# Hybrid decoder step on one Trainium2 core: key choice of the sample rows placed ahead of the attention's steps

## The chip, the cores and the metric

The kernel runs on one core of one Trainium2 chip. The metric is the device time of one execution in microseconds (us); less is better. Five engines work beside each other: TensorE (PE; its weight loads are PEld in the rows), VectorE (DVE), ScalarE (ACT), GpSimd (POOL) and SyncE (SP, which here only issues transfers). Each engine takes its own instructions strictly in the order in which they were written into its stream, and waits on semaphores for the others.

## What is computed

One layer of a decoder, for a prompt of 512 rows and for 32 sample rows (8 sequences of 4) that share all weights. Cut to what matters:

```python
h = rmsnorm(x, norm_mix_g)
q, k, v, qi, ki, wi, xl, gl, ga, gb = split_cols(h @ w_in, IN_SPLITS)
q, k = rope(q), rope(k)
# attend: indexer scores -> top-256 keys of each row -> softmax attention on these keys only
y_a = attend(q, k, v, qi, ki, wi) @ w_proj_a
y_b = (rg_lru(causal_dwconv(xl)) * gelu(gl)) @ w_proj_b
x = x + (sigmoid(ga) * y_a + sigmoid(gb) * y_b) @ w_out
h = rmsnorm(x, norm_ffn_g)
ua, ub = split_cols(h @ w_up, (D_FF, D_FF))
x = x + (gelu(causal_dwconv(ua)) * ub) @ w_down
```

For a sample row `attend` picks 256 of 4096 cached keys by score, gathers their K and V rows (8 heads of 64) from a paged cache in DRAM, and attends to them and to the new rows of its own sequence.

## The kernel before

All large products are made in split precision: an operand is cut into a high and a low fp32r half (`split_act`, line 150 ff., for activations; `load_w`, line 161 ff., for weights: SP loads at L163, ACT casts at L166, DVE subtracts at L167), and three matmuls are added.

The order of the work is set by a tile scheduler: each piece of code has a priority (`tc.high_priority(n)`; more is earlier) and every engine's stream is written by these priorities as far as data allow. The places that matter here, in order of time:

- 200 to 365 us: q, k, v and index columns of the prompt (L232 to L234, priority PRIO) while DVE sorts the sample rows' scores for the 256 largest, 32 rounds of L782 and L784 (PRIO // 10).
- 300 to 420 us: the prompt's attention (PRIO // 3, the last unit 4 * PRIO): products with split keys (L545), scores and softmax (L950 on DVE, L955 and L959 on ACT), transposes (L965), products with V (L980). The gate rows and `w_proj_b` (L247 to L249, PRIO // 6) fill PE between its steps.
- The choice (L805 to L840, PRIO // 10): DVE compares all scores with the 256th (L810, L811), ranks ties by a scan (L813), PE counts (L815, L816), DVE selects (L818 to L823), a second count and scan number the keys (L825 to L829), ACT packs them (L830 to L832); SP writes the table `cbd` to DRAM (L834) and reads it back in another layout as `M` (`cw<-cbd`, L836); DVE takes the ends `se` from it (L838).
- The sample rows' q, k and v columns (L842 to L860, PRIO // 10): `sample_cols` loads four 512 KB pieces of `w_in` (L274, tiles `cg`) and makes 32 fp32 matmuls (L281; each shows as two in the profile's counts); q and k get rope (L376 to L380), a copy in DRAM (`qsd` for q) and transposes.
- 423 to 452 us: `w_proj_a` (L1022 to L1024, 3 * PRIO), eight blocks of 12 matmuls, each closed by DVE (L1025, L1026, L157). After each block stands one step of the generator `choose` (L866 to L890, PRIO // 10), whose 8 matmuls (L878) turn `M` into row numbers with DVE's L869, L870 and L882 to L889.
- 453 to 504 us: `w_out` (L1280 to L1282) and the sums with x (L1295).
- POOL gathers K and V rows by these numbers (L1055); it also makes the power in the second norm's rsqrt (L175), in one stream.
- From 504 us: the second norm (L183 to L192, transposes L202), then `w_up` and `w_down` (L260 to L262), between whose blocks the sample rows' attention is pinned step by step (L1082 to L1091, L1138), and the tail.

The step that hands the choice on to the gathers is:

```python
for ft in range(8):
    ...
    split_act(mhi[:, ft, :SEQ], mlo[:, ft, :SEQ], sg, 0.5)
    with tc.high_priority(PRIO // 10 - 3 * PRIO):
        next(chosen, None)
```

Of the kernel before, what the change touches and what calls it, by code (L numbers as in the profile page):

```python
# [96 lines left out]
def build(tc, I, O, dbg=None, mark=lambda n: None):  # L97
    nc = tc.nc
    V, S, T, G = nc.vector, nc.scalar, nc.tensor, nc.gpsimd
# [8 lines left out]
    def pool(stack, name, bufs, **k):  # L108
        return stack.enter_context(tc.tile_pool(name=name, bufs=bufs, **k))

    def maker(p, tag):
        return lambda shape=(128, 512), dt=F32: p.tile(list(shape), dt, tag=tag, name=nm(tag))

    with outer:
# [8 lines left out]
        PC = maker(pool(outer, "pc", 2, space=PSUM), "pc")  # L123
# [14 lines left out]
        def C(name, lo=0, hi=None):  # L138
            o, w = _OFF[name]
            return (cmk if name in _MASKS else cst)[:, o + lo:o + (w if hi is None else hi)]  # L140

        ident = C("ident")
# [3 lines left out]
        PRIO = 100000  # L146
# [149 lines left out]
        CW = maker(pool(mix, "cw", 6), "cw")  # L296
# [47 lines left out]
        b = PC()  # L344
# [24 lines left out]
        def rope(dst, src, n, t, nh, mk=None, adder=None):  # L369

            cs = C("cos", t * 64, t * 64 + 64)[:n, None, :].to_broadcast([n, nh, 64])
            sn = C("sin", t * 64, t * 64 + 64).rearrange("p (a d) -> p a d", a=2)[:n, None].to_broadcast([n, nh, 2, 32])
            t1, t2 = (mk or PW)(), (mk or PW)()
            a = t1[:n, :nh * 64].rearrange("p (h d) -> p h d", h=nh)
            b = t2[:n, :nh * 64].rearrange("p (h d) -> p h d", h=nh)
            V.tensor_tensor(a, src, cs, op=ALU.mult)  # L376
            V.tensor_tensor(b.rearrange("p h (a d) -> p h a d", a=2),  # L377
                            src.rearrange("p h (a d) -> p h a d", a=2)[:, :, ::-1, :], sn, op=ALU.mult)
            for d in (dst if isinstance(dst, list) else [dst]):
                (adder or V).tensor_tensor(d, a, b, op=ALU.add)  # L380

        def heads(ap):
            return ap.rearrange("p (h d) -> p h d", d=64)
# [32 lines left out]
        b = PC()  # L416
# [9 lines left out]
        b = PC()  # L426
# [6 lines left out]
        with tc.high_priority(3 * PRIO):  # L433
# [20 lines left out]
            for u in range(16):  # L454
# [19 lines left out]
                if g:  # L474
                    b = PA()
# [7 lines left out]
            b = PC()  # L483
# [7 lines left out]
            b = PC()  # L491
# [10 lines left out]
            qsT = mp.tile([128, 4, 32], F32, name="qsT")  # L502
            kTn = mp.tile([128, 4, 32], F32, name="kTn")
            vn = mp.tile([32, 512], F32, name="vn")
            qsd = dp.tile([NQ, 512], F32, name="qsd")

            def sample_cols(col0):
                return rows_by_columns(hs, 8, CG, w_in, col0, 8)
# [12 lines left out]
        for t in range(4):  # L521
            sl = slice(t * 128, (t + 1) * 128)
            qr = qrow[:, t]
            for c0, c1 in ((0, 256), (256, 584)):
                b = PD()[:, :c1 - c0]
# [8 lines left out]
        b = PD()  # L534
# [37 lines left out]
        with tc.high_priority(PRIO):  # L572
# [11 lines left out]
            b = PD()  # L584
# [59 lines left out]
            for k6 in range(6):  # L644
# [5 lines left out]
                b = PD()  # L650
# [98 lines left out]
        b = PD()  # L749
# [19 lines left out]
        with tc.high_priority(PRIO // 10):  # L769
            scr = CW((128, 1028), F16)  # L770

            def total(cnt, mat):
                b = PC()
                T.matmul(b[:, :1], mat, cnt, start=True, stop=True)
                return b[:, :1]


            rest, top = CG((128, 1028)), CW((128, 256))
            src = SC
            for r in range(32):  # L780
                with tc.issue_after(masked.ins):
                    V.max(top[:, 8 * r:8 * r + 8], src)  # L782
                if r < 31:
                    V.match_replace(rest, top[:, 8 * r:8 * r + 8], src, SENT)  # L784
                    src = rest


            def both(lists, n):
                other, u = CW((n, 256)), CW((n, 256))
                G.tensor_copy(other, lists[n:2 * n])  # L790
                V.tensor_tensor(u, lists[:n], other[:, ::-1], op=ALU.max)
                return u

            u = both(top, 64)
            for d in (128, 64, 32, 16, 8, 4, 2, 1):
                w = CW((64, 256))
                uv, wv = (t.rearrange("p (b a d) -> p b a d", a=2, d=d) for t in (u, w))
                for a, op in ((0, ALU.max), (1, ALU.min)):
                    V.tensor_tensor(wv[:, :, a], uv[:, :, 0], uv[:, :, 1], op=op)
                u = w  # L800
            u = both(u, 32)
            V.tensor_reduce(Ff[:32], u, axis=AX.X, op=ALU.min)
            for k in range(1, 4):
                G.tensor_copy(Ff[32 * k:32 * k + 32], Ff[:32])
        with tc.high_priority(PRIO // 10):  # L805

            eq = CG((128, 1028))
            gt = CG((128, 1028))
            cg, ce = SMC(), SMC()
            V.tensor_scalar(gt, SC, Ff, None, op0=ALU.is_gt, op1=ALU.add, accum_out=cg)  # L810
            V.tensor_scalar(eq, SC, Ff, None, op0=ALU.is_equal, op1=ALU.add, accum_out=ce)  # L811
            er = CG((128, 1028))
            V.tensor_tensor_scan(er, eq, eq, 0.0, ALU.add, ALU.max)  # L813
            b = PC()
            T.matmul(b[:, 0:1], C("sq"), cg, start=True, stop=False)  # L815
            T.matmul(b[:, 0:1], C("lq"), ce, start=False, stop=True)  # L816
            lim = SMC()
            V.tensor_scalar(lim, b[:, 0:1], -1.0, 256.0, op0=ALU.mult, op1=ALU.add)  # L818
            V.scalar_tensor_tensor(er, er, lim, eq, op0=ALU.is_le, op1=ALU.mult)
            sel = gt  # L820
            cs_ = cp.tile([128, 1], F32, name="cs_")
            V.scalar_tensor_tensor(sel[:, :1024], gt[:, :1024], 1.0, er[:, :1024], op0=ALU.mult, op1=ALU.add, accum_out=cs_)
            V.tensor_tensor(sel[:, 1024:], gt[:, 1024:], er[:, 1024:], op=ALU.add)  # L823
        with tc.high_priority(PRIO // 10):
            offs = cp.tile([128, 1], F32, name="offs")  # L825
            V.tensor_copy(offs, total(cs_, C("lq")))
            CB = CW((128, 8, 130), F16)
            V.tensor_copy(CB[:, :, 0], ptq_i)
            V.tensor_tensor_scan(eq[:, :1024], sel[:, :1024], sel[:, :1024], offs, ALU.add, ALU.max)  # L829
            S.copy(CB[:, :, 1:129], eq[:, :1024].rearrange("p (g s) -> p g s", g=8))  # L830
            S.copy(CB[:, 1:8, 129], CB[:, 0:7, 128])
            S.copy(CB[:, 0, 129:130], offs)  # L832
            cbd = dp.tile([NQ, NPG, 130], F16, name="cbd")
            nc.sync.dma_start(cbd.rearrange("q (c g) s -> c q (g s)", c=4), CB.rearrange("p g s -> p (g s)"))  # L834
            M = CW((128, 8, 130), F16)
            nc.sync.dma_start(M, cbd.rearrange("(b t) p s -> (t p) b s", b=8))  # L836
            se = cp.tile([128, 8, 2], F32, name="se")
            V.tensor_copy(se, M[:, :, 128:130])  # L838
            idx = {}
            scr2 = CW((128, 512), F16)  # L840
        with tc.high_priority(PRIO // 10):
            for col0, dstTs, rows in ((0, qsT, qsd), (512, kTn, O["k_s"])):  # L842
                b = sample_cols(col0)
                raw = CW((32, 512))
                for c in range(4):
                    S.copy(raw[:, c * 128:(c + 1) * 128], b[32 * c:32 * c + 32, :128])
                kr = CW((32, 512))
                rope(heads(kr), heads(raw), 32, 4, 8, CW)
                nc.scalar.dma_start(rows, kr)
                b = PC()  # L850
                for j in range(4):
                    T.transpose(b[:, j * 32:(j + 1) * 32], kr[:, j * 128:(j + 1) * 128], ident[:32, :32])
                S.copy(dstTs, b[:, :128].rearrange("p (k c) -> p k c", k=4))
            b = sample_cols(1024)
            for c in range(4):
                S.copy(vn[:, c * 128:(c + 1) * 128], b[32 * c:32 * c + 32, :128])
            nc.scalar.dma_start(O["v_s"], vn)
# [148 lines left out]
        with tc.high_priority(3 * PRIO):  # L1006
# [7 lines left out]
            for ft in range(8):  # L1014
# [4 lines left out]
                b = PD()  # L1019
# [462 lines left out]
        for _ in range(2):  # L1482
            raw = NM((128, 2, 512))
# [39 lines left out]
        for t in range(4):  # L1523
            b = PD()
# [8 lines left out]
            if t == 2:  # L1533
                first_half(4, NQ)
                b = PC()
# [43 lines left out]
```

## Time and profile before

| | |
|---|---|
| median of 3 runs | 1028.56 us (1028.41 to 1030.61) |
| the profiled execution: its time, its span | 1030.16 us, 1028.3 us |
| mean granted TensorE clock | 0.979 |
| PE busy | 976.0 us (95% of the span) |
| DVE busy | 719.6 us (70%) |
| ACT busy | 442.3 us (43%) |
| POOL busy | 206.2 us (20%) |

The busy shares are means over stages with different limits. PE is idle or at a lower clock in a few places only, so the time is read from those places: stretches of 25 us, then the instructions in them in order of time, with what ended the idle time ahead of each.

### The profile page before, as it was taken

How to read it: one execution, taken by the hardware profiler on the slowest of the kernel's cores; microseconds unless marked ns; L12 is line 12 of the kernel's file. 1: busy time of each engine (PE TensorE's matmuls, PEld its weight loads, DVE VectorE, ACT ScalarE, POOL GpSimd, SP SyncE). 2: the span in 40 equal slices, each digit the busy share in tenths (PEclk: the TensorE clock that was granted, in tenths of full speed). 3: DMA queues.
4: the chain of work that ended last, by engine and by line, in shares of the span. 5: the costliest groups of instructions: out<-in, count | busy, mean ns of one | idle time of the engine just before them, and what ended most of it. 6: DMA issues, size and time to landing. Idle time of an engine off the chain costs nothing.

```text
span 1028.3 us, 19018 instructions
## 1 busy us (share of the span) xinstructions
PE 976.0 (95%) x7342; PEld 800.2 (78%) x7342; DVE 719.6 (70%) x1557; ACT 442.3 (43%) x1104; POOL 206.2 (20%) x197
## 2 busy tenths in 40 slices
PE   4999999999999998899799999999999999999876
PEld 3977888987779987567588777776767889999655
DVE  5657898999999985576679878964444645554444
ACT  5233664742265555433546675642213223232233
POOL 3420000002200000004504746645651000000001
PEclk9999999999999999899889999999999999999989
DMA  7652222332332242996708887866784846764472
GB/s 265 216 159 70 84 63 73 95 107 83 123 103 84 84 130 68 287 321 214 236 29 235 277 252 233 283 204 189 241 264 157 297 125 226 235 215 152 148 245 88
DMA packets 144807, 178.95 MB, mean 174 GB/s; under 512 B 10620, under 2 KB 92668, under 8 KB 144716
## 3 DMA queue, kind: packets, MB, share of 16 engines
q1 hardware_dynamic: 119432, 109.24, 34.2%
q0 software_dynamic: 14688, 49.31, 14.2%
q10 hardware_dynamic: 10596, 19.18, 6.1%
q8 instruction: 58, 0.95, 0.4%
q14 instruction: 33, 0.27, 0.1%
HBM read 168.02 MB, written 9.68 MB: 173 GB/s over the span
## 4 chain that ended last, share of the span: by engine, by line
PE 75%; DVE 9%; issue 5%; DMA 4%; ACT 3%; POOL 3%; ACTq 0%; POOLq 0%; SPq 0%; DVEq 0%
PE pd L249 6%; PE pd L247 6%; PE pd L248 6%; PE pc L281 4%; PE pd L232 3%; PE pd L234 3%; PE pd L233 3%; POOL cg L1055 2%; PE pa L545 2%; PE pd L261 2%; PE pd L260 2%; PE pd L262 2%; PE pa L260 2%; PE pa L261 2%; PE pa L262 2%
## 5 line engine op out<-in xcount | busy, mean ns | idle before, releaser
L166 ACT CAST wh<-wr 128x1024 fp32r<-128x1024 f32 (+1 forms) x126 | 125.0, 993 | 219.2 <-PE pd L234 60.6
L167 DVE TENSOR_TENSOR wl<-wr,wh 128x1024 fp32r<-128x1024 f32 (+1 forms) x126 | 145.5, 1155 | 97.5 <-ACT wh L166 96.8
L247 PE MATMUL pd<-hhi,wh 128*128 128x256 f32 (+1 forms) x384 | 113.7, 296 | 0.1
L249 PE MATMUL pd<-hhi,wl 128*128 128x256 f32 (+1 forms) x384 | 112.7, 294 | 0.0
L248 PE MATMUL pd<-hlo,wh 128*128 128x256 f32 (+1 forms) x384 | 112.3, 293 | 0.0
L1055 POOL DMA_INDIRECT cg<-in_cache_k_dram,idx x64 | 76.0, 1188 | 151.8 <-DVE cw L870 94.9
L249 PEld LDWEIGHTS pd<-hhi,wl 128*128 128x128 f32 x384 | 72.3, 188 | 4.5 <-issue 4.0
L247 PEld LDWEIGHTS pd<-hhi,wh 128*128 128x128 f32 x384 | 72.3, 188 | 3.3 <-issue 1.8
L248 PEld LDWEIGHTS pd<-hlo,wh 128*128 128x128 f32 x384 | 72.3, 188 | 2.8 <-issue 2.7
L1055 POOL DMA_INDIRECT cg<-in_cache_v_dram,idx x48 | 55.0, 1146 | 28.5 <-ACT junk L1087 14.8
L175 POOL TENSOR_TENSOR smn<-smn,mhalf 128x1 f32<-128x1 f32 (+1 forms) x15 | 10.8, 722 | 241.0 <-DVE smn L1515 200.2
L261 PE MATMUL pd<-mlo,wh 128*128 128x512 f32 (+1 forms) x136 | 53.4, 393 | 0.1
L262 PE MATMUL pd<-mhi,wl 128*128 128x512 f32 (+1 forms) x136 | 53.2, 391 | 0.0
L260 PE MATMUL pd<-mhi,wh 128*128 128x512 f32 (+1 forms) x136 | 53.2, 391 | 0.0
L260 PE MATMUL pa<-mhi,wh 128*128 128x512 f32 (+1 forms) x136 | 52.6, 387 | 0.0
L262 PE MATMUL pa<-mhi,wl 128*128 128x512 f32 (+1 forms) x136 | 52.2, 384 | 0.0
L261 PE MATMUL pa<-mlo,wh 128*128 128x512 f32 (+1 forms) x136 | 52.2, 384 | 0.0
L1087 ACT ACTIVATE junk<-cg 128x64 f16<-128x64 f32 x160 | 41.0, 256 | 24.5 <-DVE cg L1082 11.7
L380 POOL TENSOR_TENSOR pw<-pw,pw 128x512 f32<-128x512 f32 x8 | 11.2, 1398 | 192.9 <-DVE pw L377 189.2
L1082 DVE TENSOR_TENSOR cg<-cg,xb 128x1024 f32<-128x1024 f32 x32 | 38.5, 1217 | 7.2 <-DMA cg<-in_cache_k_dram,idx 3.7
L782 DVE MAX8 cw<-cg 128x8 f32<-128x1028 f32 x32 | 39.3, 1227 | 0.3
L784 DVE MATCH_REPLACE8 cg<-cw,cg 128x1028 f32<-128x1028 f32 x31 | 37.6, 1212 | 0.0
(586 smaller groups left out, 2720.7 us busy)
## 6 DMA issues: line engine op xcount, KB each, us to landing
wr<-in_w_up_dram SPq DMA_DIRECT2D x48, 512.0 KB
wr<-in_w_in_dram SPq DMA_DIRECT2D x36, 512.0 KB
sw<-in_w_up_dram SPq DMA_DIRECT2D x32, 512.0 KB
wr<-in_w_down_dram SPq DMA_DIRECT2D x20, 512.0 KB
xb<-qsd ACTq DMA_DIRECT2D x32, 256.0 KB
sw<-in_w_down_dram SPq DMA_DIRECT2D x16, 512.0 KB
cg<-in_w_in_dram SPq DMA_DIRECT2D x12, 512.0 KB
wr<-in_w_out_dram SPq DMA_DIRECT2D x8, 512.0 KB
```

The costliest lines, as they stand in the source:

```text
L166: S.copy(hi, raw)
L167: V.tensor_tensor(lo, raw, hi, op=ALU.subtract)
L247: T.matmul(b, hi[:, k, :], a_hi[:, k, c0:c1], start=k == 0, stop=False)
L248: T.matmul(b, hi[:, k, :], a_lo[:, k, c0:c1], start=False, stop=False)
L249: T.matmul(b, lo[:, k, :], a_hi[:, k, c0:c1], start=False, stop=k == nk - 1)
L260: T.matmul(b[:, c0:c1], hi[:, k, :], a_hi[:, k, c0:c1], start=k == 0, stop=False)
L261: T.matmul(b[:, c0:c1], hi[:, k, :], a_lo[:, k, c0:c1], start=False, stop=False)
L262: newest[0] = T.matmul(b[:, c0:c1], lo[:, k, :], a_hi[:, k, c0:c1], start=False, stop=k == 7)
L281: m = T.matmul(b[32 * c:32 * c + 32, :128], a_s[:, k, :], rows[k - k0][:, c * 128:(c + 1) * 128], start=k0 == 0 and k == order[0], stop=k1 ...
L782: V.max(top[:, 8 * r:8 * r + 8], src)
L1055: G.indirect_dma_start(out=dst[j], out_offset=None, in_=src, in_offset=IndirectOffsetOnAxis(ap=idx[q // 16, q % 4][:, j, q // 4 % 4:q // 4 ...
L1087: S.activation(junk, kt[:, j, h * 64:(h + 1) * 64], AF.Copy, accum_out=sT[:, g, j, q16, h:h + 1])
```

## The change

The code that picks the keys (L805 to L840) gets priority PRIO // 2 in place of PRIO // 10, which is above that of the prompt's attention (PRIO // 3). The loop over q and k columns becomes a function, `sample_heads`; its call for the q columns stands ahead of the choice (still PRIO // 10), the k and v columns stay behind it. No computation is added or removed. From L856 on a line of the changed kernel is 3 higher than before (L878 becomes L881); within the choice L815, L816 become L829, L830, and L838 becomes L852.

```diff
+        def sample_heads(col0, dstTs, rows):
+            b = sample_cols(col0)
+            raw = CW((32, 512))
+            for c in range(4):
+                S.copy(raw[:, c * 128:(c + 1) * 128], b[32 * c:32 * c + 32, :128])
+            kr = CW((32, 512))
+            rope(heads(kr), heads(raw), 32, 4, 8, CW)
+            nc.scalar.dma_start(rows, kr)
+            b = PC()
+            for j in range(4):
+                T.transpose(b[:, j * 32:(j + 1) * 32], kr[:, j * 128:(j + 1) * 128], ident[:32, :32])
+            S.copy(dstTs, b[:, :128].rearrange("p (k c) -> p k c", k=4))
         with tc.high_priority(PRIO // 10):
+            sample_heads(0, qsT, qsd)
+        with tc.high_priority(PRIO // 2):
 
             eq = CG((128, 1028))
...
-        with tc.high_priority(PRIO // 10):
+        with tc.high_priority(PRIO // 2):
             offs = cp.tile([128, 1], F32, name="offs")
...
         with tc.high_priority(PRIO // 10):
-            for col0, dstTs, rows in ((0, qsT, qsd), (512, kTn, O["k_s"])):
-                b = sample_cols(col0)
...
+            sample_heads(512, kTn, O["k_s"])
             b = sample_cols(1024)
```

PE, the first count of the choice. Before, it stands behind the last matmuls of the filler (tile `pd_5083`), next to the last attention unit (`pa_5163`):

```order
L247 MATMUL pd_5083<-hbhi,wh_5086 128x288
L248 MATMUL pd_5083<-hblo,wh_5086 128x288
L249 MATMUL pd_5083<-hbhi,wl_5087 128x288
L815 MATMUL pc_3129<-smc_3123,cst 128x1
L816 MATMUL pc_3129<-smc_3124,cst 128x1
L545 MATMUL pa_5163<-khi,pw_5160 128x256
```

Now it stands some 100 rows earlier on PE, at the seam of two filler blocks (`pd_4989` and `pd_5024`):

```order
L968 MATMUL pa_4324<-cst,pw_4241 128x128 x4
L249 MATMUL pd_4989<-hbhi,wl_4993 128x288
L815 MATMUL pc_3174<-cst,cw_3167 128x32
L829 MATMUL pc_3188<-smc_3182,cst 128x1
L830 MATMUL pc_3188<-smc_3183,cst 128x1
L247 MATMUL pd_5024<-hhi_135,wh_5028 128x256
```

The count moved over the last gate and `w_proj_b` blocks, and a transpose of the sample rows' q (`pc_3174`) stands just ahead of it.

DVE, the last attention unit (`pw_5160` is its split q, `pw_5177` its scores). Before, the second scan of the choice (L829) stands in it:

```order
L950 ISA sma_5178 128x1
L826 COPY offs<-pc_3139 128x1
L952 TENSOR_SCALAR sma_5179<-sma_5178 128x2
L829 SCALAR_TENSOR_TENSOR cg_3121<-cg_3122,offs 128x1024
L956 RECIPROCAL sma_5181<-sma_5180 128x2
L950 ISA pw_5190,sma_5191<-pa_5164,cst 128x128
```

Now the taking of `se` stands there, ahead of the split of q, and then the k columns' rope and the first step of `choose`:

```order
L154 TENSOR_TENSOR yalo<-qT,yahi 128x4x128 x2
L852 CAST se<-cw_3209 128x16
L154 TENSOR_TENSOR yalo<-qT,yahi 128x4x128
L154 TENSOR_TENSOR pw_5160<-qT,pw_5160 128x256
L959 RECIPROCAL sma_5151<-sma_5150 128x2
L376 TENSOR_TENSOR cw_3261<-cw_3255,cst 32x512
L377 TENSOR_TENSOR cw_3262<-cw_3255,cst 32x512
```

The select and scan of the choice left this stretch, and a wait for the read of `cbd` (tile `cw_3209` is `M`) came into it.

POOL, the gathers ahead of the second norm's first power (`smn_6061`), as a piece of the difference:

```order
+L1058 DMA cg_5861<-in_cache_k_dram,idx_5339 128x512 x2
+L1058 DMA cg_5907<-in_cache_k_dram,idx_5391 128x512 x2
 L175 TENSOR_TENSOR smn_6061<-smn_6059,mhalf 128x1
-L1055 DMA cg_5907<-in_cache_k_dram,idx_5391 128x512 x2
 L175 TENSOR_TENSOR smn_6088<-smn_6086,mhalf 128x1
```

Two gathers that stood behind the first power stand ahead of it; otherwise POOL's order is as it was.

## Rows read from the trace of the kernel before

**Rows 1.** The page: busy time, share of the span and instructions of each engine.

```profile
PE 976.0 (95%) x7342; PEld 800.2 (78%) x7342; DVE 719.6 (70%) x1557; ACT 442.3 (43%) x1104; POOL 206.2 (20%) x197
```

**Rows 2.** Busy time by stretch of 25 us: engines, granted clock, DMA share, GB/s.

```profile
225.00:250.00 25.00, 23.65 (x105) 18.61 (x104) 24.36 (x40) 5.37 (x6) 5.23 (x4) 1.00 0.30 86
400.00:425.00 25.00, 17.60 (x157) 12.46 (x157) 13.61 (x44) 13.42 (x44) 0.00 (x0) 0.80 0.57 177
425.00:450.00 25.00, 25.00 (x176) 17.35 (x178) 18.51 (x34) 9.54 (x19) 0.00 (x0) 1.00 1.00 334
500.00:525.00 25.00, 18.35 (x110) 14.33 (x109) 19.62 (x85) 12.45 (x47) 7.86 (x10) 0.73 0.32 96
```

**Rows 3.** DVE in order of time: start, us, engine, line [idle <-releaser].

```profile
383.33 2.29 DVE L813 TENSOR_TENSOR_SCAN cg<-cg 128x1028 f32<-128x1028 f32 x1
```

**Rows 4.** The choice on PE and DVE, same view, at the attention's end.

```profile
404.13 0.28 PE L815 MATMUL pc<-smc,cst 128*128 128x1 f32 x2
...
406.00 1.28 DVE L819 SCALAR_TENSOR_TENSOR cg<-cg,smc,cg 128x1028 f32<-128x1028 f32 x1
...
409.34 1.22 DVE L822 SCALAR_TENSOR_TENSOR cg<-cg,cg 128x1024 f32<-128x1024 f32 x1
...
411.55 2.35 DVE L829 TENSOR_TENSOR_SCAN cg<-cg,offs 128x1024 f32<-128x1024 f32 x1
```

**Rows 5.** The same view of PE: last attention unit, q columns, first w_proj_a.

```profile
409.47 0.79 PE L545 MATMUL pa<-khi,pw 64*128 64x256 f32 x4 [1.81 <-DVE pw L154]
...
414.24 1.93 PE L281 MATMUL pc<-cg,hs 128*32 128x128 f32 x30 [2.00 <-DMA cg<-in_w_in_dram]
...
422.72 0.72 PE L1022 MATMUL pd<-yahi,wh 128*128 128x512 f32 x2 [1.11 <-ACT yahi L153]
```

**Rows 6.** The same view of SP: the table written and read back.

```profile
416.47 0.61 SPq L834 DMA_DIRECT2D cbd<-cw  x1
...
426.26 0.37 SPq L836 DMA_DIRECT2D cw<-cbd  x1
```

**Rows 7.** The same view of DVE: se taken.

```profile
432.91 0.17 DVE L838 CAST se<-cw 128x16 f32<-128x16 f16 x1
```

**Rows 8.** The same view of PE: v columns inside w_proj_a.

```profile
449.32 1.08 PE L281 MATMUL pc<-cg,hs 128*32 128x128 f32 x32
```

**Rows 9.** The chain that ended last, in w_out: start, us, engine, line.

```profile
495.12 0.23 PE pd L1282
495.35 0.23 PE pd L1280
```

**Rows 10.** Groups on DVE from 453 to 526 us: count, busy us, mean ns.

```profile
L882 DVE TENSOR_SCALAR_CACHE_REDUCE cw<-pc,cst 128x127 f16<-128x127 f32 x32 | 9.5, 342 | 0.0
...
L1082 DVE TENSOR_TENSOR cg<-cg,xb 128x1024 f32<-128x1024 f32 x3 | 3.6, 1219 | 2.9 <-DMA cg<-in_cache_k_dram,idx 2.9
L1044 DVE COPY cw<-qsT 64x16 f32<-64x16 f32 x16 | 2.8, 176 | 0.2
```

**Rows 11.** POOL in order of time: gathers and the first power.

```profile
474.95 0.99 POOL L1055 DMA_INDIRECT cg<-in_cache_k_dram,idx  x1 [94.85 <-DVE cw L870]
...
488.52 1.96 POOL L1055 DMA_INDIRECT ft<-in_cache_v_dram,idx  x1 [0.30 <-issue]
...
502.99 0.95 POOL L1055 DMA_INDIRECT cg<-in_cache_k_dram,idx  x1 [0.30 <-issue]
504.00 0.57 POOL L175 TENSOR_TENSOR smn<-smn,mhalf 128x1 f32<-128x1 f32 x1
```

**Rows 12.** DVE in order of time: the first mean of squares of the second norm.

```profile
497.41 0.15 DVE L176 TENSOR_SCALAR smn<-smn 128x1 f32<-128x1 f32 x1
```

**Rows 13.** PE in order of time from the end of w_out.

```profile
504.53 0.63 PE L878 MATMUL pc<-cw,cw 32*128 32x128 f16 x8
506.39 1.09 PE L202 MATMUL pa<-cst,yn 128*128 128x128 f32 x8 [1.24 <-DVE yn L192]
...
526.53 0.39 PE L260 MATMUL pa<-mhi,wh 128*128 128x256 f32 x1
```

More of the change, by code (lines that the diff above doesn't have):

```diff
@@ L841, in build @@
         with tc.high_priority(PRIO // 10):
-            for col0, dstTs, rows in ((0, qsT, qsd), (512, kTn, O["k_s"])):
-                b = sample_cols(col0)
[L844 to L853, printed above, removed]
+            sample_heads(512, kTn, O["k_s"])
             b = sample_cols(1024)
```

## The prediction

> **What bounds the kernel now.** I read the page first. PE is busy for 976.0 us, 95% of the span [rows 1], and the change adds and removes no work, so only the places where PE stands still or runs at its lower clock can give time, and only places where PE is full can take it. The stretches of 25 us show them [rows 2]: 400 to 425 us (PE 17.60 of 25, granted clock 0.80) and 500 to 525 us (18.35, clock 0.73; a mean of 0.73 is a mixture of the two levels, 1.2 and 2.4 GHz). In 225 to 250 us PE has 1.35 us free, with DVE at 24.36 of 25. In 425 to 450 us PE has none.
>
> Then I read each place in order of time. The choice has its tie scan on DVE at 383.33 [rows 3], yet its first count on PE comes at 404.13 [rows 4]: its data have been there for 18.5 us, and it stands behind the filler in PE's stream. So its select, second select and second scan (406.00, 409.34, 411.55: 1.28 + 1.22 + 2.35 = 4.85 us of DVE, [rows 4]) fall into the attention's last unit, where PE starves (409.47, 414.24 and 422.72 all follow a wait, [rows 5]). From there the delay is handed on: the table goes out at 416.47 and is read back from 426.26 [rows 6], `se` is taken at 432.91 [rows 7], and the first gather starts at 474.95 [rows 11]. So gathers run on until 503.94 on POOL, and the second norm's first power stands behind them at 504.00 [rows 11], though its mean was there at 497.41 + 0.15 = 497.56 [rows 12]. PE ends `w_out` at 504.5, waits for the normalized rows at 506.39, and reaches steady FFN work only at 526.53 [rows 13]: 22.0 us, in which DVE also does the late steps of `choose`. That hole is what the change can close.
>
> **The change part by part.**
>
> (a) *q columns ahead.* 32 matmuls, 64 in the profile's count. 32 of that count last 1.08 us [rows 8], so 2.2 us, now among the prompt's q columns near 247 us, where PE has 1.35 us free in 25. Their four loads are issued by SP behind a weight load, at about 240 us by the order, and the last one is used first; the one row of such a wait is 2.00 us [rows 5]. Bounds 0.9 (the free time covers the rest) and 4.2. I take +2. The rope falls beside the attention, where DVE has room.
>
> (b) *The attention's tail.* The 4.85 us of DVE leave it. In come the taking of `se`, the k columns' rope, the first `choose` operations, and k and v columns on PE in place of the q columns, with their loads. The gain is at most 4.9. The loss hangs on the table: with the count near 389 us (the end of its filler block) the table is written at about 400.5; before, 16.4 us passed from its issue to `se` [rows 6, 7]. The same delay would put `se` at 416.9, and behind `se` on DVE stands the split of q for the last unit, which PE used at 409.47 [rows 5]: +7.4. Before, however, the read stood behind other transfers on SP and DMA was full (share 1.00, [rows 2]); now it stands ahead of them. Bounds -4.9 and +7.4; I take 0.
>
> (c) *k and v columns leave the full stretch* behind 422.72. 128 of the profile's count at 1.08 / 32 us each [rows 8]: 4.3 us less; both bounds are this, as PE had no idle time to hide them [rows 2]. I take -4.
>
> (d) *`choose` matmuls enter it.* Before, some 40 of them ran in the hole behind `w_out`; 8 last 0.63 us [rows 13], so +3 in `w_proj_a` and `w_out`.
>
> (e) *DVE beside `w_proj_a` and `w_out`.* From the first block to the third weight split of `w_out`, PE has by the new order 149 large matmuls at 0.23 us [rows 9] and 56 small: 34.9 + 4.4 = 39.3 us. DVE was busy 18.51 of 25 there [rows 2], or 29 us of 39. The order adds 23 counts of `choose` (0.34), 3 K products and 2 equally long reductions (1.22 each), 16 copies (0.18) [rows 10], 7.8 + 6.1 + 2.9 = 16.8 us, less some 2 us of k rope: 44 us. So DVE comes some 5 us late with a weight split. Bounds 0 (overlapped issue makes a count cheaper than its row) and +8; I take +4.
>
> (f) *The hole behind `w_out`.* `choose` is done in step with the blocks, so the first gather starts some 12 us of DVE work after 422.7, near 436, and the 22 gathers ahead of the first power, 0.95 + 0.30 us each [rows 11], end near 464, long before 497.6. The two that moved ahead of the power cost nothing under that cover; without it, 2.5 us. The hole keeps its own PE work: four times 1.09 us of transposes [rows 13] and 24 matmuls of half the width of `w_out`'s, 0.115 us each (an estimate from [rows 9]), 2.8 us. So at most 22.0 - 4.4 - 2.8 = 14.8 us go; at least 504.00 - 497.56 = 6.4 go, the wait of the power alone. With the path from the last sum to the last transposes still there, I take -12.
>
> Sum: 2 + 0 - 4 + 3 + 4 - 12 = -7 against the profiled execution, 1030.16: 1023. That execution lies 1.6 us above the median of 1028.56, so on the median's footing the forecast is **1021.5 us**. What is late next is the last row tile of the norm, then the FFN's own stalls.
>
> **Rivals.**
>
> *The gathers are slow beside a busy DVE, and still stand before the power.* In favour: where DVE was full, gathers of 1.96 us stand beside those of 0.95 [rows 11]. Against: 22 at 1.96 + 0.30 us take 50 us, from 436 to 486, in time for 497.6; it decides only if the first comes after 448. Then the power stays late, (f) keeps only the cleared `choose` steps, 12 - 6.4 = 5.6, and the time is 1028. The Trainium skill, "SBUF — State Buffer", section "SBUF: two separate sides", says that GpSimd cannot write the descriptors of its transfers while VectorE holds their shared port pair, and gives 3100 ns for a transfer that takes 620 ns alone; the 1.96 us rows agree in kind, not in size. By the page's figure, as an estimate, 22 gathers would take 68 us, end at 504, and the power would come no earlier than before.
>
> *Slower: the read of the table holds the attention's last unit.* One place, `se` on DVE ahead of the last split of q; on SP the loads of the v columns stand behind the same read. If it lands as late as it did (+7.4 in (b)), q's loads are late too (4.2 in (a), 2.2 more) and PE spends longer at the lower clock (2 more, an estimate from the 0.80 in [rows 2]), the sum is -7 + 7.4 + 2.2 + 2 = +4.6: 1033. It decides from about 7 us of lateness, `se` at 416.5. For it: the order and the 16.4 us. Against: that time held a queue that is now behind the read.
>
> *DVE takes the bound of `w_proj_a` and `w_out`.* (e) at +8 and (f) at its least: 2 - 4 + 3 + 8 - 6.4 = +2.6, 1031. For it: 44 us against 39. Against: later weight splits leave DVE room again before the norm.
>
> *The FFN gives it back.* The steps of the sample rows are pinned between its blocks and still want the same gathers; starting earlier, PE waits there instead. Half of the 7: 1025; all: 1028.5. Against: as many gathers are ahead of the norm as before.
>
> That the change does not do what it says is excluded for the order, which shows the count moved; that it moves no wait is the last rival.
>
> **How the numbers follow.** A difference under 0.2%, 2.1 us, cannot be told from no change here. Forecast (1012 to 1026): 0.60. Slow gathers: 0.05. Table: 0.15. DVE: 0.10. FFN: 0.10. Faster takes the forecast, half of the FFN's chance and a third of the gathers' and DVE's: 0.70. Slower takes the table's and a third of DVE's: 0.18; the rest, 0.12, is the same. The best sum, with every term at its gain, is 0.9 - 4.9 - 4.3 + 3 + 0 - 14.8 = -20, the worst beyond +10; neither end needs all its terms at once, so the range is 1011 to 1032, which cuts off half of the table's chance and little else.
>
> **What would show it.** PE's count near 389 us; `cbd` near 400 and `se` before 410; no select or scan of the choice after 404; first gather at 430 to 445; the first power within 1 us of its mean; the hole from `w_out`'s end to steady FFN at 8 to 12 us in place of 22.0, with the clock at 1.00 soon after. It is wrong if the attention's last products wait for `se`, if PE waits for `w_out`'s weight splits by over 8 us, or if the power still starts right behind a gather.

## The result and the profile after

Measured side by side, the changed kernel takes 1024.36 us (median of 5 runs, 1020.53 to 1025.65) and the kernel before 1030.07 us (1028.41 to 1030.74): a ratio of 0.994, interval 0.9922 to 0.9959, so 4 to 8 us faster. The forecast was 1021.5 in 1011 to 1032. The profiled execution of the changed kernel takes 1021.81 us, span 1020.0, granted clock 0.987; against the profiled one of before, 1030.16 and 1028.3, that is 8.3 us less. It lies 2.5 us under its own median, so the account below is of 8.3 us, while by the medians the change is worth 5.7. What follows reads these two traces.

The page: the same instructions, and PE 9.2 us less busy than in [rows 1], though it has the same matmuls; that fits the higher clock of 500 to 525 us below.

```profile
PE 966.8 (95%) x7342; PEld 796.3 (78%) x7342; DVE 720.1 (71%) x1557; ACT 441.4 (43%) x1104; POOL 208.9 (20%) x197
```

Busy time by stretch, columns as in [rows 2], of the changed kernel:

```profile
400.00:425.00 25.00, 17.82 (x224) 13.50 (x223) 12.34 (x46) 15.06 (x50) 0.00 (x0) 0.86 0.55 164
425.00:450.00 25.00, 23.47 (x114) 16.89 (x111) 18.12 (x65) 11.08 (x39) 4.55 (x5) 0.93 0.55 163
450.00:475.00 25.00, 19.33 (x93) 13.66 (x92) 22.55 (x65) 11.67 (x54) 17.96 (x16) 1.00 1.02 383
475.00:500.00 25.00, 24.14 (x112) 18.71 (x111) 14.58 (x39) 12.40 (x39) 1.89 (x2) 1.00 0.73 245
500.00:525.00 25.00, 23.81 (x146) 20.32 (x145) 16.57 (x37) 9.69 (x17) 2.22 (x4) 1.00 0.13 37
```

500 to 525 us, which stood at 18.35 us and clock 0.73, is repaired. A new weak stretch stands at 450 to 475 us: PE 19.33 of 25 at the full clock, with DVE at 22.55 and the DMA engines at a share of 1.02.

In order of time (start, us, engine, line, idle before and its releaser), the choice and the attention's last unit, PE, DVE and SP of the changed kernel:

```profile
390.62 0.38 PE L829 MATMUL pc<-smc,cst 128*128 128x1 f32 x2
...
398.35 2.35 DVE L843 TENSOR_TENSOR_SCAN cg<-cg,offs 128x1024 f32<-128x1024 f32 x1
...
402.75 0.61 SPq L848 DMA_DIRECT2D cbd<-cw  x1
...
410.66 0.37 SPq L850 DMA_DIRECT2D cw<-cbd  x1
...
413.82 0.17 DVE L852 CAST se<-cw 128x16 f32<-128x16 f16 x1 [4.39 <-DMA cw<-cbd]
414.51 0.42 DVE L154 TENSOR_TENSOR pw<-qT,pw 128x256 fp32r<-128x256 f32 x1
...
414.98 0.79 PE L545 MATMUL pa<-khi,pw 64*128 64x256 f32 x4 [5.10 <-DVE pw L154]
...
426.56 0.73 PE L1025 MATMUL pd<-yahi,wh 128*128 128x512 f32 x2 [1.11 <-ACT yahi L153]
```

The count is 13.5 us earlier than in [rows 4] and the second scan ends before 401. But `se` waits 4.39 us for the read of the table, the split of q stands behind it, and PE waits 5.10 us for that split where it waited 1.81 [rows 5]. `w_proj_a` starts at 426.56, 3.84 us later.

POOL of the changed kernel, the gathers and the first power of the second norm, and PE's first steady FFN product:

```profile
444.23 1.14 POOL L1058 DMA_INDIRECT cg<-in_cache_k_dram,idx  x1 [66.84 <-DVE cw L885]
...
467.10 1.65 POOL L1058 DMA_INDIRECT cg<-in_cache_k_dram,idx  x1 [0.30 <-DVE sT L1094]
...
481.21 0.94 POOL L1058 DMA_INDIRECT cg<-in_cache_k_dram,idx  x1 [8.68 <-ACT junk L1090]
482.46 0.95 POOL L1058 DMA_INDIRECT cg<-in_cache_k_dram,idx  x1 [0.30 <-issue]
502.39 0.57 POOL L175 TENSOR_TENSOR smn<-smn,mhalf 128x1 f32<-128x1 f32 x1 [18.99 <-DVE smn L183]
...
520.70 0.39 PE L260 MATMUL pa<-mhi,wh 128*128 128x256 f32 x1
```

The gathers end at 483.4, and the power, which stood behind one in [rows 11], now has 18.99 us of idle POOL before it. The last `w_out` matmul ends at 512.8, and steady FFN work comes 7.9 us later, in place of 22.0 [rows 13].

PE's waits from 427 to 515 us (us in total, times, longest) say why 450 to 475 us is weak:

```profile
PE pa L1284 <- DVE wl L167: 1.8, 1, 1.8
PE pc L881 <- ACT slot L890: 1.5, 1, 1.5
PE pa L1283 <- ACT wh L166: 1.4, 2, 0.8
PE pd L1025 <- ACT yahi L153: 1.1, 1, 1.1
PE pd L1027 <- DVE wl L167: 0.9, 2, 0.7
PE pc L881 <- DVE slot L889: 0.8, 1, 0.8
```

Both casters of the weights (ACT `wh`, DVE `wl`) are late, and both slot steps of `choose`. From the first `w_proj_a` matmul to the start of the last of `w_out` ("the stage" from here on) it takes 85.8 us, before 81.5.

What the stage is made of can be counted on PE, each row from its start to the start of the next, less the idle time (from the first start to the last end, 81.9 us before and 86.3 now). The k and v columns, with two groups of transposes (of q and k), took 8.0 us before and none now; `choose` 2.3 and 5.3; the large matmuls 70.9 and 72.5; eight transposes of the second norm, which stood behind `w_out`, 0 and 0.8; two small groups (L902, L903) 0 and 0.7; idle time 0.6 and 6.9. The columns were dear because they stood in pieces between the large matmuls. Here, before, ten of their count hold PE for 0.55 us until the next row starts, where [rows 8] has 32 in one piece of 1.08:

```profile
429.13 0.62 PE L281 MATMUL pc<-cg,hs 128*32 128x128 f32 x10
429.68 0.50 PE L1022 MATMUL pd<-yahi,wh 128*128 128x512 f32 x1
```

And the stage of the changed kernel begins at the lower clock. Its large matmuls start 0.43 us apart until 430.4 and 0.23 apart behind it; the granted clock is 0.59 from 426.5 to 430.6 and 0.99 in the 4.4 us that follow. Before, they started 0.23 apart from 423.8 on, at a clock of 1.00.

```profile
428.31 0.63 PE L1025 MATMUL pd<-yahi,wh 128*128 128x512 f32 x1
428.74 0.63 PE L1026 MATMUL pd<-yalo,wh 128*128 128x512 f32 x1
...
431.02 0.40 PE L1026 MATMUL pd<-yalo,wh 128*128 128x512 f32 x1
431.25 0.39 PE L1027 MATMUL pd<-yahi,wl 128*128 128x512 f32 x1
```

### The profile page after: what moved, and what is told of

The parts are those of the page before. It is cut to its first block, busy times and chain, and to the rows that moved or that the text cites. A ratio compares the mean times of both kernels' runs of the same rounds, so it can differ in the third digit from the quotient of the medians.

```text
span 1020.0 us, 19017 instructions
## 1 busy us (share of the span) xinstructions
PE 966.8 (95%) x7342; PEld 796.3 (78%) x7342; DVE 720.1 (71%) x1557; ACT 441.4 (43%) x1104; POOL 208.9 (20%) x197
## 4 chain that ended last, share of the span: by engine, by line
PE 77%; DVE 8%; DMA 6%; issue 3%; ACT 3%; POOL 1%; SPq 0%; ACTq 0%; POOLq 0%; DVEq 0%
PE pd L249 7%; PE pd L247 7%; PE pd L248 7%; PE pc L281 3%; PE pd L232 3%; PE pd L234 3%; PE pd L233 3%; PE pa L545 2%; PE pd L260 2%; PE pd L261 2%; PE pd L262 2%; PE pa L260 2%; PE pa L262 2%; PE pa L261 2%; PE pc L448 2%
## 5 line engine op out<-in xcount | busy, mean ns | idle before, releaser
L166 ACT CAST wh<-wr 128x1024 fp32r<-128x1024 f32 (+1 forms) x126 | 125.0, 993 | 225.3 <-PE pd L234 59.8
L249 PE MATMUL pd<-hhi,wl 128*128 128x256 f32 (+1 forms) x384 | 112.6, 294 | 0.0
L1058 POOL DMA_INDIRECT cg<-in_cache_k_dram,idx x64 | 80.7, 1261 | 126.0 <-DVE cw L885 66.8
L249 PEld LDWEIGHTS pd<-hhi,wl 128*128 128x128 f32 x384 | 72.2, 188 | 3.7 <-issue 3.0
L1058 POOL DMA_INDIRECT cg<-in_cache_v_dram,idx x48 | 51.3, 1068 | 26.5 <-ACT junk L1090 12.6
L1090 ACT ACTIVATE junk<-cg 128x64 f16<-128x64 f32 x160 | 41.0, 256 | 33.3 <-DVE cg L1085 15.6
```

The costliest lines, as they stand in the source:

```text
L166: S.copy(hi, raw)
L249: T.matmul(b, lo[:, k, :], a_hi[:, k, c0:c1], start=False, stop=k == nk - 1)
L1058: G.indirect_dma_start(out=dst[j], out_offset=None, in_=src, in_offset=IndirectOffsetOnAxis(ap=idx[q // 16, q % 4][:, j, q // 4 % 4:q // 4 ...
L1090: S.activation(junk, kt[:, j, h * 64:(h + 1) * 64], AF.Copy, accum_out=sT[:, g, j, q16, h:h + 1])
```

## The experiments

Ratios are to the kernel before in the same series, with 95% intervals. Times inside come from each kernel's profiled execution; one execution differs from the next by several us (the twelve of e1 lie between 1020.06 and 1033.48), so stages are compared inside executions, and small differences between kernels are left open.

**Which half of the change does it?** `e1_priority_only` is the kernel before with only the two priorities of the choice raised; `e2_q_columns_only` is the changed kernel with the choice back at its old priority.

```diff
-        with tc.high_priority(PRIO // 10):
+        with tc.high_priority(PRIO // 2):
```

> The priority of the choice alone, q columns left where they were in the program (behind the choice). Theory: the gain comes from the hole behind w_out, and that needs only the early choice; so the first gather stands near 440 us, the hole is 8 to 10 us, and the time is 1020 to 1027, with no q columns among the prompt's q columns and all three sets of columns in the attention's tail. Rival: the q columns are needed ahead (K products wait for q rows), then over half of the gain is gone, 1027 to 1030.

Measured: 1025.25 us, 0.9963 (0.9939 to 0.9986). The count comes at 384.06, `se` at 409.23 after a wait of 5.53 us, and PE waits 6.26 us: for ACT's half of q's split (L153), which stands behind a softmax step that waits 5.55 us for DVE, which stands at `se`. Hole from `w_out` to steady FFN 9.7 us; stage 83.4 us.

> The q columns ahead alone, choice at its old priority. In the order the first count stands early all the same, and the taking of se stands behind the last unit's split of q. Theory: the count's place decides, so the hole closes as in the change, and PE's wait of 5.1 us for the last split of q is gone (at most 2 us left): 1017 to 1025, the same as the change or up to 5 us better. Rival, that the priority is what gives the time: 1028 to 1031.

Measured: 1027.79 us, 0.9979 (0.9963 to 0.9996). The count is early in this kernel as well (390.87): to write the q columns ahead of it moves it, without the priority. Only the scan and the table stay late (407.55, 411.89), `se` falls behind the split (421.94), and PE waits 2.68 us for the split. The first gather comes at 445.79, the first power has 18.42 us of idle POOL before it, and the hole is 11.3 us. So either half alone closes most of the hole, since either makes the count early; the gains do not add up, and the intervals of the two and of the whole overlap. What made the scheduler move the count in e2 was not followed.

**What holds the attention's last unit?** Three edits of the changed kernel, one each:

```diff
-            nc.sync.dma_start(cbd.rearrange("q (c g) s -> c q (g s)", c=4), CB.rearrange("p g s -> p (g s)"))
+            nc.scalar.dma_start(cbd.rearrange("q (c g) s -> c q (g s)", c=4), CB.rearrange("p g s -> p (g s)"))
...
-            V.tensor_copy(se, M[:, :, 128:130])
+            G.tensor_copy(se, M[:, :, 128:130])
...
-            nc.sync.dma_start(M, cbd.rearrange("(b t) p s -> (t p) b s", b=8))
+            nc.gpsimd.dma_start(M, cbd.rearrange("(b t) p s -> (t p) b s", b=8))
```

The first alone is `e3_table_from_act`, the second alone `e4_se_on_pool`, the second with the third `e7_table_read_on_pool`.

> The change, with the table cbd written from ACT's queue in place of SP's, where it stood behind three loads of 512 KB. Theory: the write lands 3 to 5 us earlier, se is taken at about 410 in place of 413.8, PE's wait of 5.1 us shrinks to 1 to 2 and the time by 2 to 4 us. Rival: the write shares the engines with the same loads and lands when they do; then se stays at 413 to 414 and the time is the same.

Measured: 1026.17 us, 0.9963 (0.9945 to 0.9981). The write goes out at 403.43 from ACT, the read at 410.89, `se` at 413.96. The write is issued as long after the choice's second scan as in the changed kernel (4.40 us after its start in both), and the read follows it by 7.46 us in place of 7.91. So the place in SP's queue was not what made the table late; what the 7.5 to 7.9 us between write and read consist of stays open.

> The change, with se taken by POOL in place of DVE, so that the last split of q does not stand behind it. Theory: PE's wait of 5.1 us for that split falls under 1 us; the first choose operations on DVE still wait for se, so w_proj_a starts 2 to 5 us earlier than in the change, and the time is 2 to 5 us less. Rival: the v columns' loads, which stand behind the table's read on SP, are what holds the tail; then w_proj_a starts where it did.

Measured: 1025.62 us, 0.996 (0.9941 to 0.9979). PE in order of time from the last unit on:

```profile
410.75 0.51 PE L545 MATMUL pa<-khi,pw 64*128 64x256 f32 x4 [0.54 <-DVE pw L154]
...
417.59 3.22 PE L281 MATMUL pc<-cg,hs 128*32 128x128 f32 x56 [3.21 <-DMA cg<-in_w_in_dram]
...
426.71 0.73 PE L1025 MATMUL pd<-yahi,wh 128*128 128x512 f32 x2 [1.11 <-ACT yahi L153]
```

The wait for the split shrinks from 5.10 to 0.54 us, and PE then waits 3.21 us for the loads of the columns, which stand on SP behind the same read (issued at 410.98). `w_proj_a` starts as late as before. One late transfer held two queues, and to free one of them gave nothing.

> The change, with the read of the table and the taking of se both on POOL, which has nothing else to do then, so that neither DVE nor SP stands waiting for the table. Theory: with se alone on POOL the wait moved to the v columns' loads behind the read on SP (3.2 us); now these loads go out 2 to 4 us earlier, w_proj_a starts at 421 to 424 in place of 426.6, and the time is 2 to 5 us less than the change. Rival: the loads wait for their buffers or for a full DMA, and w_proj_a starts where it did.

Measured: 1024.47 us, 0.9952 (0.9937 to 0.9968). Neither wait is left, yet `w_proj_a` starts at 425.63, only 0.9 us earlier: small waits of the softmax (1.95, 1.78 and 0.91 us) fill the place. The table now takes longer: read at 410.55, `se` at 416.67. And what was gained is lost behind it in this execution: the stage takes 90.0 us at a mean granted clock of 0.91, in the changed kernel 85.8 at 0.98. What lowered the clock was not followed. In this kernel the cure is worth no more than the noise.

`e11_priority_only_pool` puts the same two edits on e1, where the count is 6 us earlier.

> The priority alone, q columns left behind the choice, with the table's read and se on POOL. Theory: in the run with the priority alone PE waited 6.3 us for the last unit's q, which stood behind se; that goes, w_proj_a starts at 419 to 423 in place of 425.4, and the time is 2 to 5 us under that run's. Rival: the tail is held by the columns' loads, and nothing changes.

Measured: 1020.75 us, 0.9926 (0.9903 to 0.9948). PE's wait at the last unit is 0.61 us, and `w_proj_a` starts at 421.25, 4.2 us earlier than in e1: here the chain from the table was the one that ended last. At the end of `w_out` 2.3 us of it are left (506.98 against 509.23), as the stage is longer (85.3 us against 83.4). Run again beside other kernels:

> The fastest version so far once more, as a neighbour of the other two on the same chip: priorities alone, table read back and its ends taken by POOL. If its lead is real, ratio 0.990 to 0.995 again and 2 to 4 us below the changed kernel's 1024.4; if it was a lucky draw, about 0.995 to 0.997.

Measured: 1021.31 us, 0.9907 (0.9873 to 0.9941). Its lead over the kernel before is clear of the noise. Its lead over the changed kernel, some 3 us, is one between separate series, and the intervals meet: it is not shown.

**Is it the early count that closes the hole?** `e8_all_columns_ahead` moves the k and v columns ahead of the choice too; the count then stands behind the filler, at 420.74.

```diff
             sample_heads(0, qsT, qsd)
+            sample_heads(512, kTn, O["k_s"])
+            b = sample_cols(1024)
+            for c in range(4):
+                S.copy(vn[:, c * 128:(c + 1) * 128], b[32 * c:32 * c + 32, :128])
+            nc.scalar.dma_start(O["v_s"], vn)
```

> The change, with the k and v columns ahead of the choice too. In the order their buffers push the choice back: its first count stands behind the filler again, at its new priority. Theory: the count's place decides, not its priority; so the first gather comes after 470, the first power stands behind a gather again, and the time is 1026 to 1032, the change's gain gone. Rival: the priority or the q columns' place is worth the time by itself: 1018 to 1025.

Measured: 1025.25 us, 0.997 (0.9955 to 0.9985). POOL around the first power:

```profile
497.98 0.95 POOL L1057 DMA_INDIRECT cg<-in_cache_k_dram,idx  x1 [0.30 <-issue]
498.98 0.57 POOL L175 TENSOR_TENSOR smn<-smn,mhalf 128x1 f32<-128x1 f32 x1
```

The power stands right behind a gather again, and the hole is 24.2 us (`w_out` ends at 498.0, steady FFN at 522.21). That part of the theory holds. The time was wrongly expected: it stands at the rival's edge. With most of the columns out of it and no early gathers in it, the stage took 75.8 us, 5.7 less than before, and that is worth about as much as the hole would have been. So e8 shows what opens and closes the hole, and also that the hole is not the only way to this time.

**Why did the stage grow to 85.8 us?** First suspect: the steps of `choose` come too dense. `e5_choose_half_rate` takes one only after every second block.

```diff
-                    next(chosen, None)
+                    ft % 2 and next(chosen, None)
```

> The change, with a step of choose behind every second block of w_proj_a only; the other four are drained at w_out. Theory: from the first w_proj_a matmul to the last of w_out the change takes 85.8 us against 81.5 before, because DVE comes late with weight splits and PE waits for them and for the counts (6.4 us in all); with half the steps there these waits fall under 3 us, the stretch to 81 to 84, and the time by 0 to 4 us, as the 22 gathers still end before the power. Rival: the stretch is long because of the choose matmuls on PE itself; then it stays at 85 to 86.

Measured: 1026.12 us, 0.9957 (0.9942 to 0.9972), and the stage 84.4 us, between what theory and rival expected, with the same kind of waits (7.2 us on PE). ACT now stands 14.3 us at weight casts for loads of `w_out` (1.6 in the changed kernel), so this run brings in a wait of its own. Fewer steps of `choose` alone do not cure the stage; how much `choose` adds to it is not shown.

Second suspect: the three steps of the sample rows' attention that stand in the first half of `w_out`. They run L1090 on ACT, in whose stream the next weight cast (L166) comes behind. ACT of the changed kernel, in order of time:

```profile
467.96 0.26 ACT L1090 ACTIVATE junk<-cg 128x64 f16<-128x64 f32 x1 [5.55 <-DMA cg<-in_cache_k_dram,idx]
470.14 0.26 ACT L1090 ACTIVATE junk<-cg 128x64 f16<-128x64 f32 x1 [1.82 <-DMA xa<-in_x_prompt_dram]
...
474.96 1.05 ACT L166 CAST wh<-wr 128x1024 fp32r<-128x1024 f32 x1
```

`e13_no_steps_in_w_out` leaves these steps to the places between the FFN's blocks, in the changed kernel; `e14_best_no_steps` does so in e11.

```diff
-                    if c == 0 and ks[0]:
+                    if False:
                         with tc.high_priority(PRIO // 10 - PRIO // 3):
                             next(chain)
```

> The changed kernel, but the three steps of the sample rows' attention that stand in the first half of w_out are left to the places between the FFN's blocks. Theory: the stage from the first w_proj_a matmul to the last of w_out grew to 85.8 us because these steps' K rows come late through a full DMA, and ACT (which waits 5.6 us for them ahead of a weight cast) and DVE hold the weights back; without them the stage takes 80 to 83 us, the PE waits near 470 us shrink below 2 us in sum, and the time falls by 1 to 3 us against the changed kernel, unless the FFN takes the steps back. Rival: the early gathers' traffic itself delays the weight loads; then the stage stays at 84 to 87 us with ACT waiting for w_out's loads in place of the K rows, and the time stays.

Measured: 1025.77 us, 0.9958 (0.9927 to 0.9989).

> The fastest version so far (priorities alone, the table read back and its ends taken by POOL), with the same three steps left out of w_out. Theory that the steps cause the long stage: first w_proj_a to last w_out 80 to 83 us in place of 85.4, time 1018 to 1020. Rival that the gathers' traffic does it: 84 to 87 us, time as with the steps, 1020 to 1022, or later by what the FFN pays for them.

Measured: 1023.98 us, 0.9929 (0.9903 to 0.9956). The stage takes 79.6 us in e13 and 82.2 in e14 (in e15, its neighbour with the steps, 87.0). The stretch from 450 us of e13, then two stretches of e14:

```profile
450.00:475.00 25.00, 23.43 (x123) 17.19 (x123) 23.86 (x90) 14.50 (x53) 16.57 (x15) 1.00 0.99 371
...
450.00:475.00 25.00, 25.00 (x125) 18.21 (x123) 19.99 (x79) 11.30 (x38) 14.18 (x13) 1.00 1.01 372
475.00:500.00 25.00, 25.00 (x116) 20.06 (x115) 14.80 (x38) 10.35 (x27) 1.13 (x2) 1.00 0.48 156
```

By this one edit PE goes from 19.33 of 25 us to 23.43 in e13 (DMA share 1.02 and 0.99), and from 23.59 in e11 and 22.36 in e15 to 25.00 in e14 (1.02, 1.00 and 1.01). Over the whole stage its idle time goes from 6.9 us to 1.8, and from 2.6 to none, with the same matmuls of `choose` in it. So a full share of the DMA engines is not by itself what starved it. Taking the steps out is what helped, and the waits that they put into ACT and DVE ahead of weight casts are the likely cause. But without them 16 gathers in place of 22 come ahead of the power, and these runs do not separate the two. And the time did not fall. From steady FFN to the last L249 product on `pd` it takes 397.1 us in the changed kernel, 405.6 in e13 and 407.4 in e14. PE's waits of e13 from 520 to 930 us, and POOL at the sample rows' own norm in it:

```profile
PE pc L208 <- DVE cg L192: 5.2, 1, 5.2
PE pc L281 <- DMA cg<-in_w_out_dram: 1.8, 1, 1.8
...
825.69 0.57 POOL L175 TENSOR_TENSOR smn<-smn,mhalf 32x1 f32<-32x1 f32 x1 [13.06 <-DVE smn L183]
```

The three steps are missing at the end: the sample rows reach their norm at 825.69, 9 us behind the prompt's last FFN product (816.79), so that PE has no FFN block left to run beside it; in the changed kernel at 809.97, 13 us ahead of that product (823.12). PE waits 5.2 us for the norm, and the granted clock is 0.91 in the 50 us from 825. `e16_steps_made_up` is e14 with four steps more in two groups of FFN blocks.

```diff
-                for _ in range(n // 2):
+                for _ in range(n // 2 + (f0 in (4, 8))):
```

> The version without the three steps in w_out, but two of the FFN's groups of blocks (f0 of 4 and 8) take one step more at each of their four half down-projections, so that the sample rows are done when the FFN ends. Theory: what the dropped steps gained ahead of the norm was paid back near 825 us, where the sample rows' own norm came 16 us later and PE waited 5.2 us for it (plus 2.5 us for loads and a stretch at clock 0.91 to 0.96); with the steps made up, that wait is gone, the stage keeps its 82 us, and the time is 1014 to 1019. Rival: the FFN has no room for more steps per block (loads or DVE late there); then PE waits between 575 and 675 us by as much and the time is 1020 to 1024.

Measured: **1016.3 us** (1014.83 to 1020.16), before 1030.62; 0.987 (0.9849 to 0.9891), the best of all. Stretches, and POOL at the sample rows' norm:

```profile
450.00:475.00 25.00, 25.00 (x125) 18.22 (x124) 19.49 (x75) 11.32 (x37) 13.53 (x13) 1.00 1.00 375
...
775.00:825.00 50.00, 50.00 (x376) 40.72 (x375) 25.80 (x51) 12.46 (x17) 3.11 (x5) 1.00 0.66 220
825.00:875.00 50.00, 50.00 (x518) 48.94 (x518) 28.84 (x74) 16.17 (x33) 0.00 (x0) 1.00 0.63 201
...
799.03 0.57 POOL L175 TENSOR_TENSOR smn<-smn,mhalf 32x1 f32<-32x1 f32 x1 [11.55 <-DVE smn L183]
```

The stage keeps 82.4 us, the wait for the sample rows' norm is gone, and the FFN part takes 400.6 us. Against e14 the gain is clear (the intervals 0.9849 to 0.9891 and 0.9903 to 0.9956 do not meet). Against e11 and e15, which keep the steps in `w_out`, it is not: the interval of e15 meets that of e16, and the three profiled executions take 1018.59, 1018.72 (e11) and 1019.44 (e15).

## Why the prediction was right, point by point

The hole, which was the heart of the prediction, closed as it said. The total lies near the forecast also by luck: terms (b), (c) and (e) were off, and (c) against the other two. Of the three signs of being wrong that the prediction names, one came: the attention's last products wait for `se`.

- (a) q columns ahead, +2: the last filler product of the attention comes at 406.21 after 404.00, +2.2. Right. (Between two matmuls of the prompt's q columns around the place, 243.64 to 270.31 before and 242.80 to 272.38 now, it is +2.9: this execution came there 0.8 us earlier.)
- (b) attention's tail, 0: +1.6 (`w_proj_a` 3.84 later, less the 2.2 of (a)), inside its bounds. The step that failed is "`se` before 410": it came at 413.82. From the write's issue to `se` it took 11.1 us in place of the 16.4 that served as the upper bound. The prediction hoped for less because the read had stood behind other transfers and DMA was full. But the share of 1.00 is that of 425 to 450 us, and 9.8 of the 16.4 us passed ahead of it, from the write's issue to the read's, at a share of 0.57 (400 to 425). That part shrank only to 7.9; the rest, from the read to `se`, halved from 6.6 to 3.2. So the slower rival's mechanism was there, the 5.10 us wait of PE for the split included, 2.7 us short of its turning point, 416.5. Given that wait, the term should have been set above 0; e1 and e11 show what it is worth where nothing else holds the tail, e4 and e7 that in the changed kernel other waits stand behind it.
- (c), (d), (e), columns out, `choose` matmuls in, late weights, together +3: the stage grew by 4.3. That this is close is in part luck, as the count of the stage above shows. (c) said -4, with both bounds there; the columns with the transposes had cost 8.0 us, as all but 32 of the 128 stood in pieces of 2 to 12, and the one row that was taken for the price is the one of 32. (d) said +3, and `choose` grew by 3.0. (e) said +4, and PE's idle time grew by 6.3, inside its bounds. Not in the sum were +1.6 for the large matmuls, which begin at the lower clock behind the longer wait of (b), and +1.5 for small matmuls that came in. The reason in (e) was incomplete too. It counted DVE's operations and left out ACT, which waited 5.55 us for K rows in the changed kernel. e13 and e14 show that without the sample rows' three steps (and the six gathers that go with them) most of the idle time is gone.
- (f) the hole, -12: 22.0 to 7.9, -14. Right, near its upper bound of 14.8; 0.8 of it is transposes that now run inside `w_out` and count in the stage. The clock of 1.00 that was forecast came with it. e8 confirms the cause from the other side: with a late count the power stands behind a gather and the hole is back.
- The first gather came at 444.23 instead of 436: `w_proj_a` was 3.84 us late, and the way from its start to the gather took 17.7 us instead of 13. The 22 gathers took 39 us instead of the 27.5 of the sum, since one waited 8.68 us for ACT and some were longer than 0.95 us (3.5 us in all). The margin of 18.99 us before the power covered both.

Sum of what was measured: +2.2 + 1.6 + 4.3 - 14.0 = -5.9. The FFN behind it gave 2.3 more, for a reason that was not followed (399.4 us before from steady work to the last L249 product on `pd`, 397.1 after); with 0.1 in the tail behind it that is the -8.3 between the spans.

Of the rivals, slow gathers did not come: with DVE busy for 10.00 of the 10 us from 445, gathers took 0.94 to 1.51 us. The Trainium skill, "SBUF — State Buffer", section "SBUF: two separate sides", has 3100 ns for a transfer that takes 620 ns alone, where VectorE holds the shared port pair; no gather here is lengthened by as much. But the wait itself is in the traces, and it is short because it ends with one operation of DVE. In the kernel before, the three gathers of over 1.8 us (486.41, 493.38, and 488.52 with 1.96 us, which is in [rows 11]) each start under an operation of DVE that reads two operands from SBUF:

```profile
486.18 1.21 DVE L167 TENSOR_TENSOR wo<-wr,wo 128x1024 fp32r<-128x1024 f32 x1
486.41 1.81 POOL L1055 DMA_INDIRECT ft<-in_cache_v_dram,idx  x1 [0.30 <-DVE slot L886]
...
488.45 1.22 DVE L1082 TENSOR_TENSOR cg<-cg,xb 128x1024 f32<-128x1024 f32 x1
...
493.15 1.21 DVE L167 TENSOR_TENSOR wl<-wr,wh 128x1024 fp32r<-128x1024 f32 x1
493.38 1.81 POOL L1055 DMA_INDIRECT cg<-in_cache_k_dram,idx  x1 [1.64 <-PE pa L1282]
```

They end, in order of time, 0.83, 0.81 and 0.83 us after that operation, whatever DVE does next. Over all traces of this case, from 370 to 535 us, 133 of 145 gathers that start under such an operation end 0.81 to 0.94 us after it. So a gather pays the rest of one such operation, at most some 1.2 us here, and not for all that DVE does beside it.

DVE as the bound came only as the waits above, and the FFN gave nothing back in the changed kernel. It did so in e13 and e14, where steps were left to it: the mechanism was sound, but belongs to another edit.

## What to carry to other kernels

When a small late decision feeds a long tail, follow its chain to the engine where it stands in line with work that others wait for, and move it there ahead of them; the gain is the hole at the end of the chain, not the busy time that moved. Before giving something right of way, list what stands behind its waits on every in-order queue: here one round trip through DRAM held DVE and SP at once. Freeing one of them gave nothing; freeing both brought the next stage 4.2 us forward in one kernel (e11) and 0.9 in the other (e7), where small waits took its place. Work that is moved out of a tight stage has to be made up where there is room: dropping three steps made `w_out`'s stage 3 to 6 us shorter and the FFN part 8 to 10 us longer, until four steps were placed between, which cut that loss to some 3 us.

## What the runs showed that was not expected

- The table's way through DRAM takes 7.9 us from the write's issue to that of its read and 3.2 more to `se`, with the DMA engines at a share of 0.55; the queue that it goes out on (SP or ACT) changed it by some 0.5 us.
- At a DMA share of 1.00 to 1.02 (372 to 383 GB/s) PE can be full (25.00 of 25 in e14 and e16) or short by 5.67 us (the changed kernel). The share alone told nothing of starvation.
- Small matmuls cost by the pieces that they stand in: 32 of the columns' count in one piece 1.08 us, ten between two large matmuls 0.55.
- Writing the q columns ahead, with no priority changed, moved the count by 13 us (e2).
